# Modulation vectors summed along rows, relative biases written early, and three more up tiles ahead of the expert coefficients, in a three-block model on one Trainium2 core

## Chip, cores and metric

The kernel runs on one core of one Trainium2 chip, in one launch. The metric is the device time in microseconds (us) of that core. Three runs of the kernel before gave 2993.87, 2997.18 and 3000.24 us; the median is 2997.18 us.

## The reference, cut to what matters

256 tokens of width 1024 go through three blocks. The change touches the first block and a small product that the third block uses.

```
# block 1, mixers
z = x @ w_in + b_in                                  # u, v, q, k, v_b and two gates
a = gelu(u) * (tril(w_s) mixed over tokens of LN(gelu(v)) + b_s)
l = q k^T / sqrt(128) + rel_bias[t5_bucket(t - s)]   # 8 heads, causal: NEG_INF where s > t
o = softmax(l) v_b
h = LN(alpha x + (sig(g_a) (a @ w_pa) + sig(g_b) (o @ w_pb)) @ w_out)
# block 1, expert layer: top 16 of 128 x 128 experts for each of 8 heads
hid = gelu(u_tab[experts] . h);  f = sum(gate * hid * v_tab[experts])
e = (p @ w_proj) * sigmoid(h @ w_gate + b_gate)
x = LN(alpha h + f + e)
# block 3: shifts, scales and gates, the same for all tokens
mod = silu(c) @ ada_w[l] + ada_b[l]                  # l = 0, 1: 1024 -> 6144
```

The expert layer is computed densely: all 16384 rows of the up table against all tokens (64 up tiles of 256 experts each), multiplied by a coefficient for each expert and token (zero for those not chosen), and then all 16384 rows of the down table (64 down tiles).

## The kernel before

**Arithmetic.** Most matrix products run as three fp32r products: `wsplit` (L308 to L319) loads 1 MB of weights into one of four `raw` buffers by the SP queue, ScalarE copies it to `hi` (L316), VectorE makes `lo` = raw - hi (L317), and TensorE runs hi x hi, hi x lo, lo x hi (`mm3`, L327 to L329). One chunk is 48 matmuls of 256 columns. An up tile may also be run "whole": 16 plain fp32 matmuls from `raw` (L953), which need no split; each shows as two records. 17 of the 64 up tiles are whole (`WHOLE`).

**Order of the work.** The program is written in one order, but a planner sets each engine's order: it takes instructions by priority (the order of writing) as soon as its own model of the durations says that their inputs and a buffer are there. Every engine then runs its list in order, and the issue of a DMA by ScalarE is an entry in ScalarE's list.

**Mixers of block 1 (`mixers1`, L585).** The values v (four chunks, L605 to L612), layer norm statistics (L613 to L625), normalisation on VectorE (L627 to L630), u (L632 to L636), the token mixing (L645 to L653), then the relative biases: one matmul picks the bias of each distance by head (8 partitions x 256, L658), VectorE copies it into `bv` (8 x 384, masked beyond 256), a DMA writes 128 shifted copies to DRAM from these 8 partitions (`relb`, 1532 KB, L663) and a second DMA reads them back as `rel` (L667), both by ScalarE's queue. Then q and k (L671 to L680), v_b and attention, which adds `rel` (L701).

**Expert layer (`peer`, L838).** `chosen` (L857): queries and scores, then `route` (L776) for two halves of the tokens (top 16, codes; VectorE), with up tiles dealt out between its steps (`run(ups, n)`; a step of an up tile is one sixteenth of it). Then the coefficients: 64 groups of four tokens, each one `bm` (L891) and four `am` (L897) on VectorE, four fp32 matmuls (L898), a copy to `stg` (L899), and one up step; every fourth group writes 1 MB to DRAM (`coef`, L902). 18 up tiles (`GELS`) are emitted by then. `embed` (L909) computes e: one chunk of `w_pp` and four of `w_pg`. In the phase "down" (64 steps, L844 to L848) step j takes the coefficients of tile j from a `slab` (four tiles each, loaded by ScalarE's queue when the first of the four comes up, L971), multiplies (L978), splits, and accumulates down tile j in four PSUM banks; then comes up tile j + 18, and then one `ada.step()`.

**Modulation (L1390 to L1428).** `ada.start` computes silu(c) as 8 columns (L1401). Each of 48 steps loads 128 rows x 2048 columns of `ada_w` (1 MB) and adds them, times the row's silu(c), to an accumulator `adaw` of 128 x 2048 (L1413, L1415). After every eight steps `finish` sums over the partitions: 16 fp32 matmuls of one column (L1426), and adds the bias (L1428).

Of the kernel before, what the change touches and what calls it, by code (L numbers as in the profile page):

```python
# [12 lines left out]
F32 = mybir.dt.float32  # L13
# [4 lines left out]
OP = mybir.AluOpType  # L18
# [4 lines left out]
T = 256  # L23
# [3 lines left out]
LOWEST = -3.0e38  # L27
WCH = 2048
HALFCH = 1024
GELS = 18  # L30
WHOLE = 17
ADDS = 4
LNV = 8
EPS = (1e-6, 1e-5)
# [88 lines left out]
def tcol(v):  # L123

    return np.asarray(v).reshape(-1, 128).T
# [8 lines left out]
def prepare(**a):  # L134
# [6 lines left out]
    for i, n in enumerate(("u", "va", "q", "k", "vb", "ga", "gb")):  # L141
        d["w_" + n] = lay(w[:, i * D:(i + 1) * D], 256)
        if n not in ("va", "vb"):
            vec.add("b_" + n, tcol(b[i * D:(i + 1) * D]))
    d["rows"] = np.stack([b[D:2 * D], b[4 * D:5 * D], a["gmlp_ln_g"][0], a["gmlp_ln_b"][0]])
    d["gm_ws"] = np.ascontiguousarray(a["gmlp_w_s"][0].transpose(2, 0, 1)).reshape(128, -1)
    d["gm_bs"] = a["gmlp_b_s"][0].reshape(1, -1)
    d["w_pa"] = lay(a["w_proj_a"][0], 256)
# [35 lines left out]
    d["rows16"][0] = a["fox_b_f_2"][0]  # L184
    d["rows16"][1] = np.concatenate([a["m_i_bias_3"][0], a["m_f_bias_3"][0]])

    vec.add("c", tcol(a["c_3"][0]))
    for l in range(2):
        d[f"ada{l}"] = np.ascontiguousarray(a["ada_w_3"][l].reshape(KT, 128, 3, WCH).transpose(2, 0, 1, 3))
        vec.add(f"ada_b{l}", tcol(a["ada_b_3"][l]))  # L190
        vec.add(f"n1w{l}", tcol(a["norm1_w_3"][l]))
        vec.add(f"n2w{l}", tcol(a["norm2_w_3"][l]))
# [386 lines left out]
def block1(c, x, ada):  # L579
    with c.phase("mix1", 9):  # L580
        hs = mixers1(c, x)
    ada.start()
    with c.phase("peer", 0):
        return peer(c, x, hs, ada)


def mixers1(c, x):
# [36 lines left out]
    nc.vector.tensor_scalar(sc[:, :, 3:4], sc[:, :, 3:4], -0.5, 1.5, op0=OP.mult, op1=OP.add)  # L624
    nc.vector.tensor_tensor(sc[:, :, 3:4], sc[:, :, 3:4], sc[:, :, 2:3], op=OP.mult)  # L625
    lg, lb = row(2), row(3)
    for i in range(2):  # L627
        nc.vector.tensor_scalar(va[:, i], va[:, i], st[:, i, 12:13], sc[:, i, 3:4], op0=OP.subtract, op1=OP.mult)
        nc.vector.tensor_tensor(va[:, i], va[:, i], lg, op=OP.mult)
        nc.vector.tensor_tensor(va[:, i], va[:, i], lb, op=OP.add)  # L630
# [14 lines left out]
    for g in range(8):  # L645
        ps = c.ms_ps()[:, :256].rearrange("p (n t) -> p n t", n=2)
        for n in range(2):
# [5 lines left out]
        c.split(u[:, g], a[0][:, g], a[1][:, g])  # L653


    L = 383
    ps = c.ms_ps()
    nc.tensor.matmul(ps[:8, :256], c.V("rel_bias")[:32, :], c.C("onehot")[:32, :], start=True, stop=True)  # L658
    bv = c.small([384], tag="bv", bufs=1)
    nc.vector.memset(bv[:8, :], NEG)  # L660
    nc.vector.tensor_copy(bv[:8, :256], ps[:8, :256])
    scr = c.dr.tile([8, 128 * L], F32, name="relb")
    nc.scalar.dma_start(scr.rearrange("h (r l) -> h r l", l=L),  # L663
                        bv[:8, None, :L].to_broadcast([8, 128, L]))
    rel = c.big([8, 256], nm="rel")
    s = scr[:, :]
    nc.scalar.dma_start(rel, bass.AP(tensor=s.tensor, offset=s.offset + 127,  # L667
                                     ap=[[L - 1, 128], [128 * L, 8], [1, 256]]))


    q, k = c.big([KT, T], nm="q"), c.big([KT, T], nm="k")  # L671
    for j in range(4):
        ps = c.lin_chunk(d["w_q"][j], xs)
        for f in range(2):
            h = 2 * j + f
            nc.vector.tensor_scalar(q[:, h], ps[:, f], c.V("b_q")[:, h:h + 1], 128.0 ** -0.5, op0=OP.add, op1=OP.mult)
        ps = c.lin_chunk(d["w_k"][j], xs)
        for f in range(2):
            h = 2 * j + f
            nc.vector.tensor_scalar(k[:, h], ps[:, f], c.V("b_k")[:, h:h + 1], None, op0=OP.add)  # L680
    vb = c.big([2, D], nm="vb")
    bvb = row(1)
    for j in range(4):
# [154 lines left out]
def peer(c, h, hs, ada):  # L838

    scr = c.dr.tile([T // TB, 128, 128 * TB], F32, name="coef")  # L840
    ex = Experts(c, h, hs, scr)
    with c.phase("route", 2, ("r2", "gel")):
        chosen(c, h, hs, ex, scr)
    with c.phase("down", 4, ("r2", "gel")):  # L844
        for j in range(64):
            ex.down(j)
            if j + GELS < 64:
                ex.up(j + GELS)  # L848
            ada.step()
        mean = c.ms_ps()[:, :T]  # L850
        for b in range(4):
            w = h[:, 2 * b:2 * b + 2]
            c.nc.vector.tensor_tensor(w, w, ex.ys[b], op=OP.add)
            for f in range(2):
                c.rows_add(mean, w[:, f], b + f == 0, b + f == 4)
    return c.layer_norm(h, mean, c.V("ln2_g"), c.V("ln2_b"), c.V("ng00"))


def chosen(c, h, hs, ex, scr):
# [26 lines left out]
    for tb in range(T // TB):  # L886
        stg = c.big([128, TB], nm="stg")
        for g in range(0, TB, 4):
            t0 = tb * TB + g
            bm = c.small([4, 128], tag="bm", bufs=3)  # L890
            nc.vector.tensor_tensor(bm, iota[:, None, :].to_broadcast([128, 4, 128]),  # L891
                                    eT[:, 1, t0:t0 + 4, None].to_broadcast([128, 4, 128]), op=OP.is_equal)
            ps = c.ac_ps()
            for i in range(4):
                am = c.small([128], tag="am", bufs=8)
                t = slice(t0 + i, t0 + i + 1)
                nc.vector.tensor_scalar(am, iota, eT[:, 0, t], gT[:, t], op0=OP.is_equal, op1=OP.mult)  # L897
                nc.tensor.matmul(ps[:, i * 128:i * 128 + 128], am, bm[:, i], start=True, stop=True)  # L898
            nc.scalar.activation(stg[:, :, g:g + 4].rearrange("p n t -> p t n"),  # L899
                                 ps.rearrange("p (t n) -> p t n", t=4), AF.Copy)  # L900
            run(ups, 1)
        nc.scalar.dma_start(scr[tb], stg.rearrange("p n t -> p (n t)"))  # L902
    run(ups, 16 * GELS)
    embed(c, h, hs)


def embed(c, h, hs):

    nc, d = c.nc, c.d  # L909
    alpha = 2.0 ** 0.25  # L910
# [5 lines left out]
    for j in range(4):  # L916
        pp = c.mm_ps().rearrange("p (f t) -> p f t", f=2)
        for k in range(2):
            for f in range(2):
                cs = slice((2 * j + f) * 128, (2 * j + f) * 128 + 128)  # L920
                c.mm3(pp[:, f], (w[k][0][:, cs], w[k][1][:, cs]), (pr[0][:, k], pr[1][:, k]), k + f == 0, k == 1,
                      skip_group_check=True)
        pe = c.small([2, T], tag="r2", bufs=6)
        nc.scalar.activation(pe, pp, AF.Copy)
        pg = c.lin_chunk(d["w_pg"][j], hs)
        sg = c.small([2, T], tag="r2", bufs=6)
        for f in range(2):
            g = 2 * j + f
            nc.scalar.activation(sg[:, f], pg[:, f], AF.Sigmoid, bias=c.V("ple_b_gate")[:, g:g + 1])
        nc.vector.tensor_tensor(pe, pe, sg, op=OP.mult)  # L930
        x = h[:, 2 * j:2 * j + 2]
        nc.vector.scalar_tensor_tensor(x, x, alpha, pe, op0=OP.mult, op1=OP.add)


class Experts:
# [26 lines left out]
    def up(self, j):  # L962
        run(self.steps(j), 2 * KT)

    def down(self, j):
        c, nc = self.c, self.c.nc
        b, o = divmod(2 * j, GRP)
        if o == 0:
            self.slabs[b] = c.big([T // TB, GRP, TB], nm="slab")
            src = self.scr[:, :, :]  # L970
            nc.scalar.dma_start(self.slabs[b].rearrange("p a b c -> p a (b c)"),  # L971
                                bass.AP(tensor=src.tensor, offset=src.offset + 2 * j * TB,
                                        ap=[[128 * TB, 128], [128 * 128 * TB, T // TB], [1, GRP * TB]]))
        g = self.gels.pop(j)
        cf = (c.small([2, T], F32R, tag="r2", bufs=6), c.small([2, T], F32R, tag="r2", bufs=6))
        for i in range(2):
# [414 lines left out]
class Modulation:  # L1391
# [1 line left out]


    def __init__(self, c, mod):
        self.c, self.mod = c, mod
        self.cond = c.keep.tile([128, KT], F32, name="cond")
        self.at, self.acc, self.late = 0, None, []

    def start(self):  # L1400
        self.c.nc.scalar.activation(self.cond, self.c.V("c"), AF.Silu)  # L1401

    def step(self):
        c, nc = self.c, self.c.nc
        lg, k = divmod(self.at, KT)
        if lg < 6:
            self.at += 1
            l, g = divmod(lg, 3)
            w = c.wraw(c.d[f"ada{l}"][g, k])
            cond = self.cond[:, k:k + 1]  # L1410
            if k == 0:
                self.acc = c.big(nm="adaw")
                nc.vector.tensor_scalar(self.acc, w, cond, None, op0=OP.mult)  # L1413
            else:
                nc.vector.scalar_tensor_tensor(self.acc, w, cond, self.acc, op0=OP.mult, op1=OP.add)  # L1415
        while self.late:
            self.finish(*self.late.pop(0))
        if lg < 6 and k == KT - 1:
            self.late.append((l, g, self.acc))

    def finish(self, l, g, acc):

        c, nc = self.c, self.c.nc
        cols = c.ms_ps()[:, :16]
        for i in range(16):
            nc.tensor.matmul(cols[:, i:i + 1], acc[:, i * 128:i * 128 + 128], c.C("one")[:, :1], start=True, stop=True)  # L1426
        o = 16 * g
        nc.vector.tensor_tensor(self.mod[:, l, o:o + 16], cols, c.V(f"ada_b{l}")[:, o:o + 16], op=OP.add)  # L1428


def modulated(c, x, sums, w, scale, shift, out=None):
# [608 lines left out]
```

## Time and profile before

| what | us |
|---|---|
| median of three runs | 2997.18 |
| the profiled execution, its own time | 2989.64 |
| its span, first to last instruction | 2987.9 |
| TensorE busy in the span | 2854.9 (96%) |
| VectorE busy | 2060.0 (69%) |
| ScalarE busy | 1547.6 (52%) |
| mixers of block 1 | 0 to about 290 |
| routing and coefficients | about 300 to 556 |
| phase "down" | about 560 to 1233 |

Times in the views are microseconds from the start of the span. A matmul's record is longer than the step from one matmul to the next, since matmuls are pipelined, so the number of records in a stretch says more than the busy time. A wait is listed as "who waited <- for whom". PEclk is the granted TensorE clock as a share of full speed (1.00 is 2.4 GHz, 0.50 is 1.2 GHz). A few per cent of the matmul records can be missing.

### The profile page before, as it was taken

How to read it: one execution, taken by the hardware profiler on the slowest of the kernel's cores; microseconds unless marked ns; L12 is line 12 of the kernel's file. 1: busy time of each engine (PE TensorE's matmuls, PEld its weight loads, DVE VectorE, ACT ScalarE, POOL GpSimd, SP SyncE). 2: the span in 40 equal slices, each digit the busy share in tenths (PEclk: the TensorE clock that was granted, in tenths of full speed). 3: DMA queues.
4: the chain of work that ended last, by engine and by line, in shares of the span. 5: the costliest groups of instructions: out<-in, count | busy, mean ns of one | idle time of the engine just before them, and what ended most of it. 6: DMA issues, size and time to landing. Idle time of an engine off the chain costs nothing. (4 is left out here: it accounts for less than half of the span.)

```text
span 2987.9 us, 51592 instructions
## 1 busy us (share of the span) xinstructions
PE 2854.9 (96%) x21106; PEld 2699.0 (90%) x21106; DVE 2060.0 (69%) x3625; ACT 1547.6 (52%) x2199; POOL 160.8 (5%) x136
## 2 busy tenths in 40 slices
PE   8799999899999999999999999989899999999998
PEld 8699988799999999987899989989899998788886
DVE  6365979776666676577555655555655696899997
ACT  5254417544444444437544464445544555777775
POOL 0000000000000000040000100000100071000000
PEclk9899999999999999999999999989999999999998
DMA  7544345677887796541354424534155432788885
GB/s 262 178 149 171 112 148 221 223 282 278 287 280 277 280 320 231 182 161 48 115 184 171 155 98 142 183 128 172 70 184 186 162 128 99 268 318 333 324 330 216
DMA packets 117709, 601.72 MB, mean 201 GB/s; under 512 B 9688, under 2 KB 45016, under 8 KB 48472
## 3 DMA queue, kind: packets, MB, share of 16 engines
q1 hardware_dynamic: 78480, 557.96, 52.1%
q10 hardware_dynamic: 38984, 40.39, 4.4%
q8 instruction: 167, 2.74, 0.4%
q14 instruction: 78, 0.64, 0.1%
HBM read 578.91 MB, written 19.39 MB: 200 GB/s over the span
## 5 line engine op out<-in xcount | busy, mean ns | idle before, releaser
L317 DVE TENSOR_TENSOR lo<-raw,hi 128x1024 fp32r<-128x1024 f32 x921 | 1130.8, 1243 | 639.0 <-ACT hi L316 635.4
L316 ACT ACTIVATE hi<-raw 128x1024 fp32r<-128x1024 f32 x921 | 966.9, 1057 | 1001.6 <-PE mm L328 519.5
L327 PE MATMUL mm<-nhi,hi 128*128 128x256 f32 x1312 | 379.5, 290 | 10.2 <-ACT nhi L491 6.8
L328 PE MATMUL mm<-nlo,hi 128*128 128x256 f32 x1312 | 379.6, 290 | 0.5 <-DVE nlo L492 0.5
L329 PE MATMUL mm<-nhi,lo 128*128 128x256 f32 x1312 | 377.3, 288 | 0.0
L329 PE MATMUL mm<-lhi,lo 128*128 128x256 f32 x1072 | 306.4, 286 | 8.3 <-DVE lo L317 8.3
L327 PE MATMUL mm<-lhi,hi 128*128 128x256 f32 x1072 | 305.9, 286 | 2.6 <-ACT lhi L454 2.3
L328 PE MATMUL mm<-llo,hi 128*128 128x256 f32 x1072 | 307.2, 287 | 0.0
L328 PE MATMUL ac<-r,hi 128*128 128x256 f32 x1024 | 294.0, 287 | 0.1
L327 PE MATMUL ac<-r,hi 128*128 128x256 f32 x1024 | 294.0, 288 | 0.0
L329 PE MATMUL ac<-r,lo 128*128 128x256 f32 x1024 | 293.3, 287 | 0.0
L327 PEld LDWEIGHTS mm<-nhi,hi 128*128 128x128 f32 x1312 | 258.5, 198 | 12.4 <-ACT nhi L491 7.6
L328 PEld LDWEIGHTS mm<-nlo,hi 128*128 128x128 f32 x1312 | 258.5, 197 | 2.4 <-DVE nlo L492 1.7
L329 PEld LDWEIGHTS mm<-nhi,lo 128*128 128x128 f32 x1312 | 258.3, 197 | 0.1
L329 PEld LDWEIGHTS mm<-lhi,lo 128*128 128x128 f32 x1072 | 207.6, 194 | 10.5 <-DVE lo L317 9.5
L327 PEld LDWEIGHTS mm<-lhi,hi 128*128 128x128 f32 x1072 | 207.7, 194 | 4.4 <-ACT lhi L454 2.9
L328 PEld LDWEIGHTS mm<-llo,hi 128*128 128x128 f32 x1072 | 207.5, 194 | 1.1 <-issue 0.7
L328 PEld LDWEIGHTS ac<-r,hi 128*128 128x128 f32 x1024 | 198.9, 194 | 0.3 <-DVE r L323 0.3
L329 PEld LDWEIGHTS ac<-r,lo 128*128 128x128 f32 x1024 | 198.7, 194 | 0.0
L327 PEld LDWEIGHTS ac<-r,hi 128*128 128x128 f32 x1024 | 198.7, 194 | 0.0
L328 PE MATMUL ac<-hlo,hi 128*128 128x256 f32 x688 | 193.0, 281 | 0.0
L327 PE MATMUL ac<-hhi,hi 128*128 128x256 f32 x688 | 192.8, 280 | 0.0
(592 smaller groups left out, 6285.3 us busy)
## 6 DMA issues: line engine op xcount, KB each, us to landing
raw<-in_moe_gu SPq DMA_DIRECT2D x88, 1024.0 KB, 6.1
raw<-in_peer_u SPq DMA_DIRECT2D x64, 1024.0 KB, 4.9
raw<-in_peer_v SPq DMA_DIRECT2D x64, 1024.0 KB, 5.1
raw<-in_ada SPq DMA_DIRECT2D x48, 1024.0 KB, 7.3
raw<-in_moe_d SPq DMA_DIRECT2D x40, 1024.0 KB, 6.2
raw<-in_up SPq DMA_DIRECT2D x32, 1024.0 KB, 4.9
raw<-in_down SPq DMA_DIRECT2D x32, 1024.0 KB, 4.9
raw<-in_ffn_gu SPq DMA_DIRECT2D x22, 1024.0 KB, 4.9
```

What stands on the lines that cost most here:

```text
L316: nc.scalar.activation(hi, raw[:, a:a + m], AF.Copy)
L317: nc.vector.tensor_tensor(lo, raw[:, a:a + m], hi, op=OP.subtract)
L327: mm(ps, w[0], x[0], start=start, stop=False, **k)
L328: mm(ps, w[0], x[1], start=False, stop=False, **k)
L329: mm(ps, w[1], x[0], start=False, stop=stop, **k)
```

## The change

Four things. (1) `ada_w` is laid out so that a partition is an output column: a step loads 128 columns x 2 x 1024 rows, and VectorE multiplies each half by silu(c), which lies along the row in all partitions, and sums along the row into one column of `mod` (`accum_out`). The accumulators, the column matmuls and `finish` are gone. silu(c) is made at the start of the phase "down" from a broadcast load of 1024 values, and the steps run beside j = 2 to 49. (2) The relative biases are computed before the normalisation of v, for all 128 partitions at once (eight matmuls of 32 rows, four copies on ScalarE), written as two DMAs from 128 partitions (1024 KB, and 508 KB of mask in rows of 127 values), and read back after q and k. (3) `GELS` 18 to 21, `WHOLE` 17 to 20: of every four groups of coefficients three run two up steps and one runs one. (4) `embed` moves into the phase "down", the slab of tile block b + 1 is loaded when block b begins, and the first one within `embed`. Wide buffers of the phase go from 4 to 3, and a scratch area for software DMA is halved.

```
-GELS = 18
-WHOLE = 17
+GELS = 21
+WHOLE = 20
...
     lg, lb = row(2), row(3)
+    L = 383
+    rows, low = c.big([8, 256], nm="relw"), c.small([L - 256], tag="bv", bufs=1)
+    nc.gpsimd.memset(low, NEG)
+    for h in range(0, 8, 2):
+        ps = c.ms_ps().rearrange("p (h l) -> p h l", h=2)
+        for i in range(2):
+            nc.tensor.matmul(ps[:, i], c.V("rel_bias")[:32, h + i:h + i + 1].to_broadcast([32, 128]),
+                             c.C("onehot")[:32, :], start=True, stop=True)
+        nc.scalar.activation(rows[:, h:h + 2], ps, AF.Copy)
+    scr = c.dr.tile([128, 8, L], F32, name="relb")
+    nc.scalar.dma_start(scr[:, :, :256], rows)
+    nc.scalar.dma_start(scr[:, :, 256:], low[:, None, :].to_broadcast([128, 8, L - 256]))
...
-    L = 383
-    ps = c.ms_ps()
-    nc.tensor.matmul(ps[:8, :256], c.V("rel_bias")[:32, :], c.C("onehot")[:32, :], start=True, stop=True)
...
-    nc.scalar.dma_start(scr.rearrange("h (r l) -> h r l", l=L),
-                        bv[:8, None, :L].to_broadcast([8, 128, L]))
-    rel = c.big([8, 256], nm="rel")
...
             nc.vector.tensor_scalar(k[:, h], ps[:, f], c.V("b_k")[:, h:h + 1], None, op0=OP.add)
+    rel = c.big([8, 256], nm="rel")
+    s = scr[:, :, :]
+    nc.scalar.dma_start(rel, bass.AP(tensor=s.tensor, offset=s.offset + 127, ap=[[8 * L - 1, 128], [L, 8], [1, 256]]))
...
-    with c.phase("down", 4, ("r2", "gel")):
+    with c.phase("down", 3, ("r2", "gel")):
+        ada.start()
+        embed(c, h, hs, ex)
         for j in range(64):
             ex.down(j)
             if j + GELS < 64:
                 ex.up(j + GELS)
-            ada.step()
+            if j > 1:
+                ada.step()
...
-            run(ups, 1)
+            run(ups, 1 if g == 12 else 2)
...
+        if j == 2:
+            ex.fetch(0)
         pg = c.lin_chunk(d["w_pg"][j], hs)
...
+        if o == 0 and j < 60:
+            self.fetch(b + 1)
...
     def start(self):
+        self.cond = c.small([D], tag="cond", bufs=1)
+        nc.scalar.dma_start(self.cond, bass.AP(tensor=src.tensor, offset=src.offset + 4 * D, ap=[[0, 128], [1, D]]))
+        nc.scalar.activation(self.cond, self.cond, AF.Silu)
     def step(self):
+        l, q = divmod(self.at, 24)
+        self.at += 1
+        w = c.wraw(c.d[f"ada{l}"][q]).rearrange("p (a k) -> p a k", a=2)
+        for i in range(2):
+            o = 2 * q + i
+            nc.vector.scalar_tensor_tensor(w[:, i], w[:, i], 1.0, self.cond, op0=OP.mult, op1=OP.mult,
+                                           accum_out=self.mod[:, l, o:o + 1])
+        if q == 23:
+            nc.vector.tensor_tensor(self.mod[:, l], self.mod[:, l], c.V(f"ada_b{l}"), op=OP.add)
```

## Rows read from the trace of the kernel before

**Rows 1.** The page's first part: busy time of each engine, its share of the span, instructions.

```profile
PE 2854.9 (96%) x21106; PEld 2699.0 (90%) x21106; DVE 2060.0 (69%) x3625; ACT 1547.6 (52%) x2199; POOL 160.8 (5%) x136
```

**Rows 2.** Stretches of the mixers stage: from and to, length, then busy time (records) of PE, PEld, DVE, ACT and POOL, granted clock, busy share of the DMA engines, GB/s.

```profile
5.00:29.00 24.00, 20.55 (x144) 20.00 (x145) 14.61 (x20) 16.66 (x23) 0.00 (x0) 1.00 1.01 408
40.00:70.00 30.00, 30.00 (x250) 29.40 (x249) 25.14 (x46) 17.02 (x28) 5.87 (x1) 1.00 0.46 168
82.30:104.40 22.10, 0.28 (x3) 0.08 (x1) 0.00 (x1) 1.09 (x2) 0.00 (x0) 0.55 0.44 92
104.40:108.40 4.00, 3.52 (x14) 3.23 (x15) 4.00 (x5) 2.81 (x3) 0.00 (x0) 0.50 1.04 345
```

**Rows 3.** Waits from 0 to 320 us: who waited for whom, us in total, times, longest.

```profile
ACT hi L316 <- DMA relb<-bv: 31.2, 1, 31.2
...
PE mm L327 <- ACT hi L316: 21.8, 1, 21.8
```

**Rows 4.** The instructions that touch `relb`, and the old bias matmul (duration in ns min/median/max, first and last start in us).

```profile
L663 ACTq DMA_DIRECT2D relb<-bv x1: 1276/1276/1276, 67.4 to 67.4; - x1
L667 ACTq DMA_DIRECT2D rel<-relb x1: 390/390/390, 102.8 to 102.8; - x1
...
L658 PE MATMUL ms<-cst,vecs x2: 374/376/378, 65.1 to 65.3; 32*8 32x256 f32 x2
```

**Rows 5.** The instructions that touch `adaw`, in the same columns.

```profile
L1426 PE MATMUL ms<-cst,adaw x192: 164/250/353, 696.1 to 1171.4; 128*128 128x1 f32 x192
L1415 DVE SCALAR_TENSOR_TENSOR adaw<-raw,cond,adaw x42: 2342/2347/2353, 600.1 to 1148.2; 128x2048 f32<-128x2048 f32 x42
L1413 DVE TENSOR_SCALAR adaw<-raw,cond x6: 1279/1281/1287, 584.2 to 1070.2; 128x2048 f32<-128x2048 f32 x6
```

**Rows 6.** TensorE in order of time at the first set of columns: start, length, what.

```profile
695.69 0.28 PE L327 MATMUL mm<-lhi,hi 128*128 128x256 f32 x1
695.81 0.28 PE L328 MATMUL mm<-llo,hi 128*128 128x256 f32 x1
...
696.06 4.12 PE L1426 MATMUL ms<-cst,adaw 128*128 128x1 f32 x32
```

**Rows 7.** Stretches of the phase "down", columns as in rows 2: one of steady work, and the stretch behind each of the six sets of columns.

```profile
600.00:692.00 92.00, 92.00 (x774) 92.00 (x773) 67.16 (x66) 43.69 (x50) 0.00 (x0) 1.00 0.83 297
...
700.10:705.70 5.60, 5.60 (x27) 5.60 (x27) 3.32 (x8) 0.37 (x1) 0.00 (x0) 0.50 0.50 171
798.00:801.40 3.40, 3.40 (x17) 3.40 (x17) 3.31 (x8) 0.00 (x0) 0.00 (x0) 0.50 0.21 60
897.00:900.40 3.40, 3.40 (x19) 3.40 (x18) 3.32 (x9) 0.00 (x0) 0.00 (x0) 0.50 1.01 381
993.50:999.40 5.90, 5.90 (x29) 5.90 (x30) 3.32 (x8) 0.44 (x1) 0.00 (x0) 0.50 0.41 144
1091.50:1095.00 3.50, 3.50 (x18) 3.50 (x18) 3.50 (x10) 0.00 (x0) 0.00 (x0) 0.51 1.00 363
1171.50:1176.90 5.40, 5.40 (x27) 5.40 (x26) 1.91 (x3) 0.00 (x0) 0.00 (x0) 0.50 0.51 164
```

**Rows 8.** Stretches of the routing (410 to 450 us, where TensorE runs whole up tiles alone), of the coefficients, and behind the wait for the first slab, columns as in rows 2.

```profile
410.00:450.00 40.00, 40.00 (x187) 35.17 (x186) 30.63 (x87) 6.46 (x9) 0.00 (x0) 1.00 0.44 150
450.00:515.00 65.00, 64.63 (x451) 58.37 (x450) 64.33 (x198) 48.25 (x52) 0.00 (x0) 1.00 0.56 209
515.00:540.00 25.00, 18.17 (x127) 15.71 (x126) 25.00 (x78) 16.10 (x16) 0.00 (x0) 1.00 0.45 185
540.00:556.00 16.00, 14.29 (x115) 13.50 (x115) 16.00 (x40) 10.44 (x11) 0.00 (x0) 1.00 0.52 198
...
572.30:576.10 3.80, 3.75 (x17) 3.75 (x18) 2.81 (x7) 0.00 (x0) 0.00 (x0) 0.50 0.73 250
```

**Rows 9.** TensorE's groups from 450 to 556 us: line, operation, out <- in, shapes, count, busy us, mean ns, idle before it and for whom.

```profile
L898 PE MATMUL ac<-bm,am 128*128 128x128 f32 x512 | 72.7, 282 | 7.7 <-DVE am L897 7.6
L953 PE MATMUL mm<-x,raw 128*128 128x256 f32 x113 | 31.7, 380 | 0.0
```

**Rows 10.** The writes of `coef` to DRAM (the issue on ScalarE's queue, first and last, and the time to landing).

```profile
L902 ACTq DMA_DIRECT2D coef<-stg x16: 326/326/333, 456.5 to 555.3; - x16
...
DMA to landing us min/median/max: 3.8/4.6/8.2
```

**Rows 11.** Waits from 540 to 580 us, columns as in rows 3.

```profile
DVE gel L978 <- DMA slab<-coef: 6.9, 1, 6.9
PE mm L329 <- DVE lo L317: 6.8, 5, 5.2
```

**Rows 12.** VectorE's groups over the whole span: the split of half a chunk, a multiply-add of 1024 columns, the read of an accumulator (count, busy us, mean ns, idle before).

```profile
L317 DVE TENSOR_TENSOR lo<-raw,hi 128x1024 fp32r<-128x1024 f32 x918 | 1129.8, 1246 | 639.0 <-ACT hi L316 635.4 <-PE mm L329 0.8
...
L1678 DVE SCALAR_TENSOR_TENSOR lg<-hf,lg 128x1024 f32<-128x1024 f32 x2 | 2.4, 1220 | 1.1 <-ACT lg L1677 1.1
...
L1530 DVE DVE_READ_ACCUMULATOR me<-ac,me 128x1 f32 x16 | 1.3, 83 | 0.0
```

**Rows 13.** A ScalarE group from 440 to 600 us: a copy of 512 columns out of PSUM, columns as in rows 12.

```profile
L924 ACT ACTIVATE r<-mm 128x512 f32<-128x512 f32 x4 | 2.4, 598 | 2.5 <-PE mm L329 2.5
```

**Rows 14.** A DMA issue of the first 75 us: a row of values broadcast to all partitions (queue, count, KB each, median us to landing).

```profile
row<-in_rows ACTq DMA_DIRECT2D x2, 512.0 KB, 10.2
```

**Rows 15.** A DMA issue from 600 to 1100 us, in the same columns: the slab loads, which read pieces of 512 bytes.

```profile
slab<-coef ACTq DMA_DIRECT2D x13, 1024.0 KB, 12.1
```

More of the change, by code (lines that the diff above doesn't have):

```diff
@@ L144, in prepare @@
             vec.add("b_" + n, tcol(b[i * D:(i + 1) * D]))
-    d["rows"] = np.stack([b[D:2 * D], b[4 * D:5 * D], a["gmlp_ln_g"][0], a["gmlp_ln_b"][0]])
+    d["rows"] = np.stack([b[D:2 * D], b[4 * D:5 * D], a["gmlp_ln_g"][0], a["gmlp_ln_b"][0],
+                          np.asarray(a["c_3"][0]).reshape(-1)])
     d["gm_ws"] = np.ascontiguousarray(a["gmlp_w_s"][0].transpose(2, 0, 1)).reshape(128, -1)
@@ L185, in prepare @@
     d["rows16"][1] = np.concatenate([a["m_i_bias_3"][0], a["m_f_bias_3"][0]])
-    vec.add("c", tcol(a["c_3"][0]))
     for l in range(2):
-        d[f"ada{l}"] = np.ascontiguousarray(a["ada_w_3"][l].reshape(KT, 128, 3, WCH).transpose(2, 0, 1, 3))
+        d[f"ada{l}"] = np.ascontiguousarray(a["ada_w_3"][l].reshape(D, 24, 2, 128).transpose(1, 3, 2, 0)).reshape(24, 128, WCH)
         vec.add(f"ada_b{l}", tcol(a["ada_b_3"][l]))
@@ L581, in block1 @@
         hs = mixers1(c, x)
-    ada.start()
     with c.phase("peer", 0):
@@ L653, in mixers1 @@
         c.split(u[:, g], a[0][:, g], a[1][:, g])
-    L = 383
-    ps = c.ms_ps()
-    nc.tensor.matmul(ps[:8, :256], c.V("rel_bias")[:32, :], c.C("onehot")[:32, :], start=True, stop=True)
[L659 to L662, printed above, removed]
-    nc.scalar.dma_start(scr.rearrange("h (r l) -> h r l", l=L),
-                        bv[:8, None, :L].to_broadcast([8, 128, L]))
-    rel = c.big([8, 256], nm="rel")
-    s = scr[:, :]
-    nc.scalar.dma_start(rel, bass.AP(tensor=s.tensor, offset=s.offset + 127,
-                                     ap=[[L - 1, 128], [128 * L, 8], [1, 256]]))
     q, k = c.big([KT, T], nm="q"), c.big([KT, T], nm="k")
@@ L900, in chosen, with embed @@
                                  ps.rearrange("p (t n) -> p t n", t=4), AF.Copy)
-            run(ups, 1)
+            run(ups, 1 if g == 12 else 2)
         nc.scalar.dma_start(scr[tb], stg.rearrange("p n t -> p (n t)"))
     run(ups, 16 * GELS)
-    embed(c, h, hs)
-def embed(c, h, hs):
+def embed(c, h, hs, ex):
     nc, d = c.nc, c.d
@@ L963, in up, with fetch @@
         run(self.steps(j), 2 * KT)
+    def fetch(self, b):
+        self.slabs[b] = self.c.big([T // TB, GRP, TB], nm="slab")
+        src = self.scr[:, :, :]
+        self.c.nc.scalar.dma_start(self.slabs[b].rearrange("p a b c -> p a (b c)"),
+                                   bass.AP(tensor=src.tensor, offset=src.offset + b * GRP * TB,
+                                           ap=[[128 * TB, 128], [128 * 128 * TB, T // TB], [1, GRP * TB]]))
     def down(self, j):
@@ L967, in down @@
         b, o = divmod(2 * j, GRP)
[L968 to L973, printed above, removed]
+        if o == 0 and j < 60:
+            self.fetch(b + 1)
         g = self.gels.pop(j)
@@ L1395, in __init__ @@
     def __init__(self, c, mod):
-        self.c, self.mod = c, mod
-        self.cond = c.keep.tile([128, KT], F32, name="cond")
-        self.at, self.acc, self.late = 0, None, []
+        self.c, self.mod, self.at = c, mod, 0
     def start(self):
-        self.c.nc.scalar.activation(self.cond, self.c.V("c"), AF.Silu)
+        c, nc = self.c, self.c.nc
+        src = c.d["rows"]
+        self.cond = c.small([D], tag="cond", bufs=1)
+        nc.scalar.dma_start(self.cond, bass.AP(tensor=src.tensor, offset=src.offset + 4 * D, ap=[[0, 128], [1, D]]))
+        nc.scalar.activation(self.cond, self.cond, AF.Silu)
     def step(self):
+        if self.at == 48:
+            return
         c, nc = self.c, self.c.nc
[L1405 to L1428, printed above, removed]
+        l, q = divmod(self.at, 24)
[7 more added lines that the diff above has]
+            nc.vector.tensor_tensor(self.mod[:, l], self.mod[:, l], c.V(f"ada_b{l}"), op=OP.add)
 def modulated(c, x, sums, w, scale, shift, out=None):
@@ L2028 @@
     arrays, vec_at = prepare(**{k: v for k, v in locals().items()})
-    nc = bacc.Bacc("TRN2", target_bir_lowering=False, num_devices=1)
+    nc = bacc.Bacc("TRN2", target_bir_lowering=False, num_devices=1, dynamic_dma_scratch_size=8192)
     dram = {k: nc.dram_tensor("in_" + k, v.shape, mybir.dt.from_np(v.dtype), kind="ExternalInput").ap()
```

## The prediction

> **What bounds the kernel now.** Over the span it is TensorE, busy 96% [rows 1]; but a busy share hides what is wasted, so I read the three stages that the change touches. In the mixers the stretches show one hole: from 82.3 to 104.4 us TensorE does nothing, and after it the clock is at 0.50 (1.2 GHz) for 4 us [rows 2]. The waits say why: ScalarE waited 31.2 us for the write of `relb` to land, because the read of `rel` stands in its list, and TensorE then waited 21.8 us for ScalarE's split [rows 3]. The write was issued at 67.4 us from 8 partitions, the read could go only at 102.8 us [rows 4]. The difference of the two waits, 31.2 - 21.8 = 9.4 us, is how far ScalarE works ahead of TensorE: a stop of ScalarE shorter than that is free here. In the phase "down" TensorE is full (92.00 of 92 us) with VectorE at 67.16, ScalarE at 43.69 and the DMA engines at 0.83 [rows 7], so there any TensorE work removed is time removed, down to the next limit. In the coefficients VectorE is full from 515 us on (25.00 of 25 us) and TensorE is not (18.17, and a record overstates its step) [rows 8].
>
> **(1) Modulation.** Removed from TensorE: six sets of 16 fp32 column matmuls, 192 records [rows 5]. One set of 32 records takes 4.12 us, standing between split matmuls that step 0.12 us (695.69 to 695.81) [rows 6]; six sets are 24.7 us. Behind each set comes a stretch at half clock, in which TensorE has work throughout. The six stretches add up to 27.2 us and hold 137 records [rows 7]; in steady work a record takes 92/774 = 0.119 us, so these would take 16.3 us: 10.9 us lost. The columns are one wide, and the clock falls right behind every set and not in the 92 us of steady work before the first, so I count the loss as theirs. Together -35.6 us.
>
> Added on VectorE: per step two multiply-adds of 1024 columns with a sum. The nearest rows are a plain multiply-add of that width, 1220 ns, and an accumulator read, 83 ns [rows 12]: 2.61 us, against (42 x 2.347 + 6 x 1.281)/48 = 2.21 us [rows 5]. VectorE needs 67.16/8 = 8.4 us per step of the loop (92 us are eight steps of 11.5 us), so 8.8 us after; TensorE's 96 matmuls take 11.4. Hidden, at 0. The loads are as many and as large.
>
> The steps now end at j = 49 while up tiles end at j = 42, so seven steps (two before) have a down tile and a modulation step alone: TensorE 48 x 0.119 = 5.7 us, VectorE two splits 2.49 [rows 12], the modulation 2.61, and 8.4 - 2.21 - 4 x 1.246 = 1.2 for coefficients and their split, in all 6.3. Five more such steps at 0.6 are 3 us, and 7 if the DMA lags as well; 0 if work done ahead covers it. I take +3.
>
> silu(c) becomes a wait: ScalarE issues a broadcast load and then the activation waits for it, with splits and embed's copies queued behind, for which TensorE waits. A broadcast row took 10.2 us to land [rows 14]; ScalarE's lead is 9.4. Ends 0 and +5 (if half the load is exposed); I take +1.
>
> **(2) Relative biases.** Removed: 22.1 us of idle TensorE, and half of its time at half clock (14 records in 4 us where 1.7 us do), about 1.7 after allowing for the 0.5 idle there: -23.8. Added on TensorE: eight fp32 matmuls of 256 columns, two records each, at 40/187 = 0.214 us a record [rows 8]: 3.4 us, less about 0.5 for the old one [rows 4]: +2.9, at a place where TensorE is full [rows 2]. ScalarE: four copies of 0.598 us [rows 13] and two issues, hidden while it is busy 17.02 of 30 us [rows 2]; VectorE loses a copy; POOL's memset has no one before it.
> The new write is of 1 MB in pieces of 1 KB and 0.5 MB in pieces of 508 bytes. Bounds for it: 1 MB in long pieces lands in 4.6 us [rows 10], 1 MB in pieces of 512 bytes in 12.1 us [rows 15], so 7 to 18 us from an issue at about 43. The planner put the old read about 4.7 us behind the write; if it pulls the new one up in the same way, ScalarE stands for at most 13 us, of which 9.4 are free. So the term lies between -20.9 and -17; emitted after q and k, it can also stand 40 us later and wait for nothing. I take -20.9.
> The Trainium skill ("DMA: Bandwidth & Descriptors", Specifications) asks for 512 bytes at least and says that shorter transfers are read, modified and written; the mask rows are 508. No row shows a price for that; twice the time for that half alone would add about 6 us to the landing, and the sum would not move unless the read stands early.
>
> **(3) Three more up tiles, whole.** TensorE's work grows: a whole tile is 32 x 0.214 = 6.8 us, a split one 48 x 0.119 = 5.7, and three tiles change kind: +3.3. They go where TensorE idles. How much idle there is: by busy time 0.4 + 6.8 + 1.7 = 8.9 us from 450 to 556 [rows 8]; by steps, 512 records of half as many columns at half of 0.214 (an estimate), 113 at 0.214 and some 60 at 0.119 [rows 8, 9] make 86 of 106 us, so 20. Dealing out 7 steps per four groups, instead of 4, gives TensorE 7 x 0.43 + 32 x 0.107 = 6.4 us against VectorE's 6.6 (106/16): nearly even, so hand-over losses appear. The gain is the idle filled less 3.3: between 0 and -16; I take -9. Routing itself is unchanged.
>
> **(4) Embed and slabs.** VectorE stood 6.9 us on the first slab, TensorE 5.4 of it at one time (6.8 in all), and 3.8 us at half clock followed (17 records, 1.8 lost) [rows 8, 11]. The read cannot begin before the last `coef` write has landed (555.3 + 4.6 [rows 10]), nor can the earlier place in the program change that; VectorE's list still holds the splits behind the multiplication. TensorE will have more embed work left by then. Ends 0 and -7; I take -3. Embed's own loads and copies are the same, moved past the load of c only. Later slabs a block ahead take away VectorE waits that TensorE never felt: 0. The smaller scratch area and the third wide buffer free room and issue nothing: 0.
>
> **Sum.** -35.6 + 3 + 1 - 20.9 - 9 - 3 = -64.5 us, from the profiled execution's 2989.6: 2925. That execution lies 7.5 us under the median of the runs shown, from which the same sum gives 2933. I forecast 2930, 2.2% faster.
>
> **Rivals.**
> *A, the bias wait only moves.* If the new write is as slow as the old (about 35 us), with the read pulled up behind it, ScalarE stands again from about 47 us and TensorE loses the same 23.8: 2954. For: the planner misjudged that very write [rows 3, 4], and the weights then move 339 to 408 GB/s before 40 us (the stretch to 29 us has 1.01 of the DMA engines [rows 2]). Against: 128 partitions instead of 8, and the place after q and k.
> *B, "down" hits DMA or VectorE.* Where up tiles have ended, a step moves 2 MB and a quarter slab, 2.36 MB in 5.7 us, 414 GB/s. Steady work needs 297 at a share of 0.83 [rows 7], and it already runs at the pace that is left when the columns go, which speaks against a limit there. If the loop slowed by 15 us in all, 2945. The trace once moved 408 GB/s for 24 us [rows 2]. By the same page of the Trainium skill (Specifications), one core's share of the memory is about 358 GB/s; that row contradicts it. By that figure a late step takes 6.6 us, and the seven would lose about 6.
> *C, slower: the sum along the row is slow.* No row has this sum at 1024 columns with both inputs in memory. VectorE has 11.4 - (8.4 - 2.21) = 5.2 us for a modulation step before it becomes the bound. To eat 64.5 us, 48 steps must exceed that by 1.34: 6.6 us, or 3.3 us for one instruction, 2.5 times the 1.30 of rows 12. At 4 us each the loop gives 48 x 2.8 = 134 us: 3000 or more. The read of 83 ns speaks against it.
>
> **How the numbers follow.** Forecast 0.70, A 0.14, B 0.11, C 0.05. Best case of my terms: -35.6 - 20.9 - 16 - 7 = -79.5, 2910 from the profiled time; the orders that the planner draws elsewhere can move some us either way: low 2904. High: A with its own spread, 2962. A change of 0.2%, 6 us, is about what runs of this kernel can tell from none. Forecast, A and B are all faster: 0.95; C splits into 0.02 same and 0.03 slower.
>
> **What would show it.** No stretch of idle TensorE between 70 and 110 us, and no wait of ScalarE on `relb` over 9 us. No matmul on `adaw`; in steady work of "down" eight steps in about 92 us with no half-clock stretch. `am` matmuls and whole tiles without gaps up to the last `coef`; a wait on the first slab of 0 to 7 us. The sum instruction at 1.2 to 1.3 us. I am wrong if the half-clock stretches stay without the columns, if a new wait of over 10 us appears before 70 us or around 560, or if VectorE ends steps of "down" last.

## The result and the profile after

The changed kernel takes 2927.91 us (median of four runs, 2925.78 to 2931.56) against 2995.52 us: 67.6 us less, ratio 0.9776 with a 95% interval from 0.9756 to 0.9796. The forecast was 2930 us. The profiled execution took 2925.78 us, its span is 2924.1 us.

Where the time went: first the page's busy times of the changed kernel, then its stretches (columns as in [rows 2]).

```profile
PE 2818.6 (96%) x20880; PEld 2666.6 (91%) x20880; DVE 2063.4 (71%) x3757; ACT 1543.8 (53%) x2196; POOL 156.8 (5%) x137
```

```profile
70.00:110.00 40.00, 40.00 (x336) 40.00 (x335) 26.65 (x37) 15.75 (x17) 0.00 (x0) 1.00 0.63 224
...
432.00:537.00 105.00, 105.00 (x746) 99.64 (x746) 104.81 (x311) 73.86 (x76) 0.00 (x0) 1.00 0.62 231
...
547.00:550.40 3.40, 0.64 (x6) 0.44 (x4) 0.00 (x0) 3.35 (x5) 0.00 (x0) 0.99 1.02 358
550.40:560.00 9.60, 5.45 (x29) 5.24 (x30) 5.94 (x12) 2.32 (x3) 0.00 (x0) 0.68 1.06 273
...
575.60:580.00 4.40, 0.89 (x8) 0.68 (x7) 2.52 (x4) 1.71 (x2) 0.00 (x0) 1.00 1.03 277
...
692.00:784.00 92.00, 92.00 (x774) 92.00 (x772) 67.57 (x90) 42.00 (x48) 0.00 (x0) 1.00 0.84 302
1060.00:1110.00 50.00, 50.00 (x422) 50.00 (x422) 43.67 (x60) 22.80 (x27) 0.00 (x0) 1.00 0.89 323
...
1080.00:1100.00 20.00, 20.00 (x171) 20.00 (x170) 18.45 (x25) 9.06 (x11) 0.00 (x0) 1.00 0.96 346
```

The hole of [rows 2] is gone: TensorE is full from 70 to 110 us. The coefficients (432 to 537 us) are now full on TensorE, not only on VectorE [rows 8]; since overlapping records can hide gaps, the part on why the prediction was right counts this again by steps. Steady work of "down" runs at the same step as before (774 records in 92 us [rows 7]), with VectorE at 67.57. What is left are the three holes near 548, 555 and 577 us, around the first slab.

Milestones make the account. The first matmuls that only block 2 has, in the kernel before and in the changed one (duration min/median/max, first and last start):

```profile
L993 PE MATMUL ms<-rraw,cst x14: 592/592/697, 1289.7 to 1342.9; 128*128 128x512 f32 x14
```

```profile
L1001 PE MATMUL ms<-rraw,cst x14: 590/593/697, 1227.6 to 1280.9; 128*128 128x512 f32 x14
```

There the changed kernel leads by 62.1 us, at the end of the span by 63.8. Two earlier milestones are read in the same way: the first expert query, and the first and last coefficient matmul, before and after.

```profile
L898 PE MATMUL ac<-bm,am x512: 272/275/377, 450.2 to 553.8; 128*128 128x128 f32 x171
...
L327 PE MATMUL mm<-lhi,hi x1072: 274/283/581, 299.9 to 1340.3; 128*128 128x256 f32 x179
```

```profile
L901 PE MATMUL ac<-bm,am x512: 270/275/275, 430.8 to 535.4; 128*128 128x128 f32 x171
...
L327 PE MATMUL mm<-lhi,hi x1024: 277/283/580, 280.1 to 1278.3; 128*128 128x256 f32 x171
```

The first expert query starts 19.8 us earlier. The coefficient matmuls end 18.4 us earlier, with three more up tiles done. So 43.7 us are gained between the last coefficient and block 2.

The new pieces, by row. The three DMAs on `relb` (first and last start, landing below), then the sum along the row:

```profile
L638 ACTq DMA_DIRECT2D relb<-bv x1: 618/618/618, 1.0 to 1.0; - x1
L637 ACTq DMA_DIRECT2D relb<-relw x1: 521/521/521, 42.8 to 42.8; - x1
L680 ACTq DMA_DIRECT2D rel<-relb x1: 393/393/393, 78.9 to 78.9; - x1
...
DMA to landing us min/median/max: 5.9/7.4/16.1
```

```profile
L1422 DVE SCALAR_TENSOR_TENSOR raw<-raw,cond x96: 1217/1221/1228, 598.2 to 1106.0; 128x1024 f32<-128x1024 f32 x96
L1422 DVE DVE_READ_ACCUMULATOR raw<-raw,cond x96: 80/83/86, 599.4 to 1107.2; 128x1 f32 x96
```

The bias rows land 5.9 us after 42.8, that is 30 us before they are read (the mask, issued at 1.0 us beside the first loads, took the 16.1); nobody waits on `relb`. The sum costs 1221 + 83 ns. And the waits from 440 to 640 us, which answer to [rows 11]:

```profile
DVE gel L986 <- DMA slab<-coef: 10.5, 2, 8.6
...
PE mm L329 <- DVE lo L317: 7.7, 2, 4.2
...
PE mm L327 <- ACT r L933: 2.8, 1, 2.8
...
ACT cond L1411 <- DMA cond<-in_rows: 1.6, 1, 1.6
```

### The profile page after: what moved, and what is told of

Its sections match the earlier page's. It is cut to its first block, busy times and chain, and to the rows that moved or that the text cites. A ratio compares the mean times of both kernels' runs of the same rounds, so it can differ in the third digit from the quotient of the medians.

```text
span 2924.1 us, 51291 instructions
## 1 busy us (share of the span) xinstructions
PE 2818.6 (96%) x20880; PEld 2666.6 (91%) x20880; DVE 2063.4 (71%) x3757; ACT 1543.8 (53%) x2196; POOL 156.8 (5%) x137
## 5 line engine op out<-in xcount | busy, mean ns | idle before, releaser
L329 PE MATMUL mm<-lhi,lo 128*128 128x256 f32 x1024 | 295.1, 288 | 7.7 <-DVE lo L317 7.7
L327 PE MATMUL mm<-lhi,hi 128*128 128x256 f32 x1024 | 294.9, 289 | 5.1 <-ACT r L933 2.8
L328 PE MATMUL mm<-llo,hi 128*128 128x256 f32 x1024 | 295.6, 289 | 0.0
L328 PE MATMUL ac<-r,hi 128*128 128x256 f32 x1024 | 288.2, 282 | 0.0
L327 PE MATMUL ac<-r,hi 128*128 128x256 f32 x1024 | 287.7, 281 | 0.0
L329 PEld LDWEIGHTS mm<-lhi,lo 128*128 128x128 f32 x1024 | 201.0, 196 | 9.0 <-DVE lo L317 8.1
L327 PEld LDWEIGHTS mm<-lhi,hi 128*128 128x128 f32 x1024 | 201.2, 197 | 6.9 <-ACT r L933 3.0
L328 PEld LDWEIGHTS mm<-llo,hi 128*128 128x128 f32 x1024 | 200.9, 196 | 1.1 <-issue 0.7
L328 PEld LDWEIGHTS ac<-r,hi 128*128 128x128 f32 x1024 | 192.9, 188 | 0.0
L329 PEld LDWEIGHTS ac<-r,lo 128*128 128x128 f32 x1024 | 192.7, 188 | 0.0
L327 PEld LDWEIGHTS ac<-r,hi 128*128 128x128 f32 x1024 | 192.7, 188 | 0.0
```

The lines of the kernel that those rows point to most:

```text
L327: mm(ps, w[0], x[0], start=start, stop=False, **k)
L328: mm(ps, w[0], x[1], start=False, stop=False, **k)
L329: mm(ps, w[1], x[0], start=False, stop=stop, **k)
```

## The experiments

Each is set against the kernel before on its own chip; a difference given in us is of the medians.

**e1, the biases alone.** The kernel before with part 2's lines only.

```
     lg, lb = row(2), row(3)
+    rows, low = c.big([8, 256], nm="relw"), c.small([L - 256], tag="bv", bufs=1)
+    nc.gpsimd.memset(low, NEG)
...
+    nc.scalar.dma_start(scr[:, :, :256], rows)
...
-    ps = c.ms_ps()
-    nc.tensor.matmul(ps[:8, :256], c.V("rel_bias")[:32, :], c.C("onehot")[:32, :], start=True, stop=True)
...
```

> The kernel before with the relative biases alone changed (part 2: computed for 128 partitions before the normalisation of v, read back after q and k); modulation, tiles and slabs as before. Theory (the wait of 31.2 us goes, the new write lands before its read): 18 to 21 us under the kernel before, no stretch of idle TensorE between 70 and 110 us, no half clock there. Rival A (the wait only moves): within 5 us of the kernel before. If the early mask write, which in the changed kernel went out at 1.0 us, costs TensorE the 2 us by which its first matmul came later there, that delay shows here too.

2975.23 against 2992.92 us: 17.7 us, ratio 0.9939 (0.9915 to 0.9962). TensorE is full where the hole was, and nothing waits on `relb`:

```profile
70.00:110.00 40.00, 40.00 (x336) 40.00 (x336) 26.73 (x39) 15.75 (x17) 0.00 (x0) 1.00 0.65 224
```

The gain is just under the 18 to 21 us expected, and its interval is 11 to 25 us; the theory holds, rival A falls. TensorE's first matmul comes at 9.2 us, late as in the changed kernel (8.5; before 6.5); see e8.

**e2, only the read moved.**

```
-    nc.scalar.dma_start(rel, bass.AP(tensor=s.tensor, offset=s.offset + 127,
-                                     ap=[[L - 1, 128], [128 * L, 8], [1, 256]]))
...
             nc.vector.tensor_scalar(k[:, h], ps[:, f], c.V("b_k")[:, h:h + 1], None, op0=OP.add)
+    nc.scalar.dma_start(rel, bass.AP(tensor=s.tensor, offset=s.offset + 127,
+                                     ap=[[L - 1, 128], [128 * L, 8], [1, 256]]))
```

> The kernel before with only the read of the biases written behind q and k in the program; the write still goes from 8 partitions at about 67 us. If the place in the program is what removes the wait: no stop of ScalarE, about 20 us under the kernel before. If the speed of the write is (the planner pulls the read up to where it believes the write has landed): ScalarE still waits 25 to 32 us for relb, TensorE idles about 20 us, and the time is within 5 us of the kernel before. I expect the second.

2990.6 us, ratio 0.9992 (0.9979 to 1.0005): no gain. Its DMAs, and its waits from 0 to 320 us:

```profile
L663 ACTq DMA_DIRECT2D relb<-bv x1: 1276/1276/1276, 67.9 to 67.9; - x1
L678 ACTq DMA_DIRECT2D rel<-relb x1: 390/390/390, 104.2 to 104.2; - x1
```

```profile
ACT hi L316 <- DMA relb<-bv: 26.3, 1, 26.3
...
PE mm L327 <- ACT hi L316: 15.6, 1, 15.6
```

Though written after q and k, the read was put in ScalarE's list only two splits later than before: four stand between the write and the read, where two did. So the place in the program alone does not remove the wait. With the new write (e1) it is gone; whether an early write from 8 partitions, or a late one from 128, would have done it was not tried.

**e3, the modulation alone.** The kernel before with the new class, its layout and its start in "down", steps from j = 0.

```
-    with c.phase("down", 4, ("r2", "gel")):
+    with c.phase("down", 3, ("r2", "gel")):
+        ada.start()
```

> The kernel before with the modulation alone changed (part 1: columns on partitions, sums along the row, silu(c) made at the start of the phase down; steps from j = 0, three wide buffers); biases, tiles and slabs as before. Theory: the 192 column records (24.7 us) and the half clock behind them (10.9 us) both go: 33 to 37 us under the kernel before, no half-clock stretch between 600 and 1180 us. Rival B/C (VectorE or the DMA takes over): under 20 us gained, VectorE at over 90% in steady work of the phase.

2961.16 us: 31.8 us, ratio 0.989 (0.9872 to 0.9908). From 692 us in steady work:

```profile
692.00:784.00 92.00, 92.00 (x774) 92.00 (x773) 67.53 (x89) 42.00 (x48) 0.00 (x0) 1.00 0.84 301
```

VectorE is at 73%, and the granted clock is 1.00 all the way from 600 to 1180 us, so in steady work B and C fall. But the median misses the expected 33 to 37 us (the interval is 27 to 38), and the trace shows why the gain can be smaller. Around the first slab TensorE stops for 7.0 and 4.8 us, 11.7 in all, counted from one matmul's start to the next; in the kernel before it is one stop of 5.4. The waits from 536 to 600 us:

```profile
PE mm L329 <- DVE lo L317: 12.8, 6, 6.7
...
DVE gel L978 <- DMA slab<-coef: 9.1, 2, 8.4
...
DVE raw L1414 <- DMA raw<-in_ada: 2.6, 1, 2.6
```

In the first gap VectorE waits 8.4 us for the slab (6.9 before [rows 11]); the load of c was issued just ahead of it. In the second it waits 2.6 us for a load of `ada_w`, with a split that TensorE needs behind it. Six slab loads go out from 553 to 603 us, three in the kernel before: the accumulators, which shared the wide buffers with the slabs, are gone.

**e4, the same columns, spread.** Two column matmuls a step instead of sixteen at once.

```
-        for i in range(16):
+        for i in range(2 * n, 2 * n + 2):
             nc.tensor.matmul(cols[:, i:i + 1], acc[:, i * 128:i * 128 + 128], c.C("one")[:, :1], start=True, stop=True)
```

> The kernel before with the 16 column matmuls of each group not in one set but two at each of the next eight steps; same number of column matmuls, everything else as before. Theory (the run of one-column matmuls is what lowers the clock): no half-clock stretch between 600 and 1180 us, 10 to 12 us under the kernel before, the 24.7 us of the records kept. Rival (the clock falls for another reason, or the lost time is only the records): the half-clock stretches stay and the time is within 4 us of the kernel before.

2980.06 us: 12.9 us (8 to 17 by the interval), ratio 0.9958 (0.9944 to 0.9973), with not one column matmul removed. The stretch from 600 to 1180 us in the kernel before and in e4:

```profile
600.00:1180.00 580.00, 578.34 (x4746) 578.13 (x4745) 397.35 (x405) 249.69 (x286) 0.00 (x0) 0.97 0.79 283
```

```profile
600.00:1180.00 580.00, 580.00 (x4876) 580.00 (x4876) 407.12 (x415) 258.44 (x295) 0.00 (x0) 1.00 0.81 288
```

So the run of narrow matmuls did lower the clock, and by the medians that is two fifths of what part 1 gains (12.9 of 31.8 us). Around the first slab this trace has one gap of 5.6 us, as before.

**e5, the tiles undone.**

```
-GELS = 21
-WHOLE = 20
+GELS = 18
+WHOLE = 17
...
-            run(ups, 1 if g == 12 else 2)
+            run(ups, 1)
```

> The changed kernel with the tile counts of before (18 up tiles emitted by the coefficients, 17 whole, one step for each group of four tokens). My prediction priced this part at 9 us, between 0 and 16; the trace of the changed kernel has the coefficients no longer than before (105 us) with three more tiles in them, so 48 x 3 split matmuls at 0.119 us leave the phase down for nothing: 17 us, less what the changed start of the phase gives back. Theory: 10 to 17 us slower than the changed kernel (2938 to 2945 us). Rival (the tiles only push the wait on the first slab about): within 5 us of it.

2945.46 us, ratio 0.9847 (0.9833 to 0.986). Against the changed kernel's ratios, 0.9776 and 0.9792 (e9), that is 0.55 to 0.71%, 16 to 21 us; in the traces block 2 starts 13.2 us later (1240.8 us). e6 to e8, which ran on the same chip as e5 and take as long as the changed kernel, had medians of 2926.96 to 2927.32 us, 18 us less. The theory holds; of its 10 to 17 us the trace is inside, the times are at the upper end or above it. From 495 us on the coefficients have the old gap, and they end no sooner (last one at 534.5 us, in the changed kernel at 535.4):

```profile
495.00:521.00 26.00, 18.85 (x129) 16.20 (x128) 26.00 (x81) 16.75 (x16) 0.00 (x0) 1.00 0.46 190
```

**e6, part 4 undone.**

```
-        embed(c, h, hs, ex)
...
+    embed(c, h, hs, ex)
...
-        if o == 0 and j < 60:
-            self.fetch(b + 1)
+        if o == 0:
+            self.fetch(b)
```

> The changed kernel with part 4 undone: embed ahead of the phase down and of the load of c, each slab loaded when its first tile comes up. My prediction gave this part 3 us of gain. The trace of the changed kernel speaks against it: TensorE idles 11.3 us in three gaps around the first slab (6 before), with 13.6 us at half clock (6.8 before), and the second slab is loaded beside the first. Theory now: 3 to 8 us faster than the changed kernel without it (2920 to 2925 us), the first slab landing sooner after its issue. Rival (as predicted): 1 to 5 us slower.

2926.96 us, ratio 0.9783 (0.977 to 0.9796): no difference from the changed kernel that these runs can tell, and the interval is 4 us to either side. My new theory, that the gaps would shrink, was as wrong as the old one. Its waits from 536 to 600 us:

```profile
DVE gel L984 <- DMA slab<-coef: 11.6, 3, 8.9
...
PE mm L329 <- DVE lo L317: 10.9, 2, 7.2
```

Counted from one matmul's start to the next, as in the expectation, the gaps make 11.5 us in two instead of 11.3 in three.

**e7, whole tiles left over for the wait.** `GELS` and `WHOLE` 22.

> The changed kernel with 22 up tiles ahead of the phase down, all 22 whole, dealt out as in the changed kernel, so that 25 of the 352 steps are left when the last coefficient group is done. A whole tile needs no split, hence neither ScalarE's nor VectorE's list. Theory (TensorE idles after the last coefficients because all it has left stands behind the wait for the first slab in VectorE's list): the left-over steps (25 x 0.43 = 10.7 us) cover that wait, the idle of 11 us falls to under 4, the half clock there goes, and the kernel is 6 to 12 us faster than the changed one (2916 to 2922 us). Rival (the DMA, at over 0.9 there, is what the stage waits for): the gaps move behind the left-over steps and the time stays within 4 us.

2927.32 us, ratio 0.9785 (0.9772 to 0.9798): no gain. The idle moved to another list: a whole tile needs no split, but ScalarE still reads its result (`gel`, L963), and that read stood behind the load of c. Waits from 536 to 600 us:

```profile
DVE gel L986 <- DMA slab<-coef: 20.4, 2, 19.3
...
PE mm L327 <- ACT gel L963: 5.2, 1, 5.2
ACT L1411 <- issue: 4.8, 1, 4.8
ACT cond L1411 <- DMA cond<-in_rows: 3.9, 1, 3.9
PE mm L329 <- DVE lo L317: 3.8, 3, 2.7
```

**e8, the mask written late.**

```
-    nc.gpsimd.memset(low, NEG)
+    nc.vector.tensor_scalar(low, rows[:, 0, :L - 256], 0.0, NEG, op0=OP.mult, op1=OP.add)
```

> The changed kernel with the mask tile made from the bias rows on VectorE instead of by POOL's memset, so that its write cannot go out before 42 us (it went at 1.0 us, ahead of the first weights). Theory (the early mask write delays the first loads): TensorE's first matmul at 6.5 us as before the change instead of 8.5 to 9, and 1 to 3 us faster than the changed kernel. Rival (the start varies by itself): first matmul and time unchanged; the mask write may also land late and hold the read.

2927.09 us, ratio 0.979 (0.9771 to 0.9809): the same. TensorE does start at 6.7 us instead of 8.5. In the eight traces with the early mask write it starts at 8.4 to 9.2 us, in the five without at 6.5 to 6.8, so that write did hold up the first loads. But the first expert query starts at 280.0 us, as in the changed kernel (280.1). In this trace a good part of the 1.8 us goes to a stretch at half clock, which the trace of the changed kernel does not have: from 16 to 20 us the granted clock is 0.74, there 1.00. Why it fell here was not tried.

**e9, e10, e11: the changed kernel again, c early, and c early with the left-over tiles.** e10 starts the modulation ahead of the routing:

```
-        eq = c.small([16, NCAND], tag="eq", bufs=2)
+        eq = c.small([16, NCAND], tag="eq", bufs=1)
...
+    ada.start()
     with c.phase("route", 2, ("r2", "gel")):
...
-        ada.start()
```

> The changed kernel once more, on the same chip as the two versions of it below, to set them against: about 2928 us, 0.977 to 0.979 of the kernel before.

> The changed kernel with silu(c) loaded and made ahead of the routing instead of at the start of the phase down (one buffer of the routing's selection instead of two makes the room). Theory (in the gap at 547 us TensorE waited 2.8 us for ScalarE's copies, which stood behind the load of c and two table loads): the first of the three gaps (3.0 us) goes, the other two stay, since they wait for the slab in VectorE's list; 1 to 4 us faster than the changed kernel of this set. Rival (the slab's landing ends the stage whatever stands before it): the gaps grow by what is removed, the time the same.

> As e10, and 22 whole up tiles ahead of the phase down, as in e7. In e7 the left-over steps ran as meant, but then TensorE waited 5.2 us for ScalarE's copy of an up tile, which stood behind the load of c (3.9 us) and its table loads. Theory: without these the left-over steps cover the wait for the slab; TensorE's gaps from 536 to 600 us fall under 5 us in all (11.3 in the changed kernel, 9.6 in e7), and the kernel is 4 to 9 us faster than the changed kernel of this set. Rival: what is saved there is paid by slower whole tiles (two more, 1.1 us each) and by slabs that land late; within 3 us.

e9: 2933.86 us, ratio 0.9792 (0.9772 to 0.9812). e10: 2931.75, 0.9798 (0.9784 to 0.9811). e11: 2928.59, 0.979 (0.9776 to 0.9804). By the ratios none can be told from another. The medians put e11 5.3 us under e9, but e9's own five runs spread over 12.1 us. In e10 the gap near 547 us goes and the next grows from 4.4 to 7.9 us; the gaps make 11.8 us in all. In e11 they make 10.1, and who waits has changed once more (536 to 600 us):

```profile
DVE gel L986 <- DMA slab<-coef: 18.5, 3, 17.4
...
PE mm L327 <- ACT r L933: 3.8, 1, 3.8
PE mm L329 <- DVE lo L317: 3.8, 4, 1.4
```

So e10's rival holds, and e11's theory falls: the gaps were to come under 5 us. Five arrangements (the changed kernel, e6, e7, e10, e11) give TensorE 9.6 to 11.8 us of gaps there. In all of them the first slab is multiplied 15 to 20 us after the last coefficient write was issued, and the lists of VectorE or ScalarE hold what TensorE needs behind it. A version that beats the changed kernel was not found.

## Why the prediction was right

**Part 1, forecast -35.6 + 3 + 1 = -31.6; e3 measured -31.8.** The columns and the clock behind them were read rightly; e4 supports the split (10.9 forecast for the clock, 12.9 measured). That the sum fits as well is in part luck. The +3 for the late steps is not in e3, whose steps begin at j = 0, and in the changed kernel it did not occur: where up tiles have ended (their last matmul starts at 1076 us), TensorE is full, with 171 records from 1080 to 1100 us, 0.117 us each. VectorE is near its limit there (18.45 of 20 us), and the DMA engines moved 346 GB/s, not the 414 of rival B. Work done ahead covered it, the lower end I had kept. In its place the start of the phase cost more than the +1 for c: the gaps around the first slab are 6.3 us longer in e3. With that, -35.6 + 6.3 gives -29.3, and from the last coefficient matmul to block 2 e3's trace is 29.4 us shorter than the one before (706.5 against 735.9). The load of c is not all of it, since e10 takes c away and keeps 11.8 us of gaps. The prediction had the change of the wide buffers at 0, because it was to "free room and issue nothing"; with the accumulators gone, the slab loads went out sooner. That their crowding makes the second gap is read from the waits of e3, not tried.

**Part 2, forecast -20.9; e1 measured -17.7 (11 to 25 by its interval), the milestone -19.8.** The bias rows landed in 5.9 us. My bounds of 7 to 18 were for both halves together; in e8, where the two writes go out within 3.3 us of each other, the second lands 11.8 us after the first was issued, inside them. The read stood far behind. Not foreseen was the start: POOL's memset, free at once, let the mask write go ahead of the first weights (e8).
The Trainium skill's 512 bytes ("DMA: Bandwidth & Descriptors", Specifications) fit e8, but e8 does not show that they are the cause: 508 KB of mask in pieces of 508 bytes took 9.1 us to land and 1024 KB in pieces of 1 KB took 8.5. Per byte that is twice the time, as my sentence on it had supposed. Both writes have 1024 pieces, though, so a fixed time for each piece would give the same. It fell outside the path.

```profile
relb<-relw ACTq DMA_DIRECT2D x1, 1024.0 KB, 8.5
relb<-bv ACTq DMA_DIRECT2D x1, 508.0 KB, 9.1
```

**Part 3, forecast -9, between 0 and -16; e5 measured 13 to 21.** This term was mis-sized. I took the middle of the range for fear of hand-over losses between VectorE and TensorE. There are hardly any: between the first and the last coefficient matmul no step from one matmul's start to the next is over 0.22 us, where in the kernel before those over 0.3 us added up to 14 us. The stage lasts 104.6 us where it lasted 103.6. The bound by steps was the value to take. It was a little high itself: the coefficient records step 0.112 us, not the estimated 0.107, which leaves 17 us of idle instead of 20, and less 3.3 that is about 14. The bound by busy time (8.9) was misleading, because a record of 282 ns covers gaps between steps of 112.

**Part 4, forecast -3, between 0 and -7; e6 measured 0, with 4 us of interval.** The prediction said that the place in the program cannot move the first read ahead of the last write's landing, and that holds. The -3 rested on TensorE having more embed work left: it had, and it stands behind the same wait. The gaps around the first slab even grew, from 5.4 us to 11.3, and one sign of the prediction failed with that: VectorE's wait on the first slab was to be 0 to 7 us and is 8.6 (10.5 with that on a later one). The growth does not come from part 4. It is there with the old tiles (e5, 10.0), with the old embed and slabs (e6, 11.5), and with part 1 alone (e3, 11.7), and it is absent with part 2 alone (e1, 5.5): it comes with part 1.

The terms sum to -31.8 - 17.7 - 13 (to 21) + 0 = -62 to -71 us, against -67.6 measured. The forecast of -64.5 came so near because its errors offset each other: parts 2 and 4 gave about 3 us less each than forecast, part 3 gave 4 to 12 more. C was right to be small: the sum took 1.30 us, just as its two rows said [rows 12].

## What to carry to other kernels

Price a stage's idle by counting steps, not by busy time, when records overlap. A DMA that reads back what another has written wants that write early and quick; moving the read in the program is not enough where a planner sets the order (e2). A change that only frees buffers is not free of effect either: here the loads that could use them went out sooner (e3). Filling an engine's idle was worth nearly its full size here until the engine was full; then the next hand-over, the first read of the coefficients, kept what was left, whichever list was cleared.

## What the runs showed of the hardware that was not expected

Sixteen matmuls of one column in a row, 4.12 us [rows 6], cost another 2 us behind them by the clock, which in the first set fell before the set had ended (0.87 from 695.9 to 700.1 us). Two of them between 96 wide ones cost nothing of that kind: e4's granted clock is 1.00 over 580 us. TensorE is busy throughout in both (578.34 and 580.00 of 580 us).

A write of 1532 KB from 8 partitions took about 35 us to land (67.4 to 102.8 us [rows 4]), one of 1024 KB from 128 partitions 5.9 us. Other traffic was not what held the first: from 91 to 102 us, when the loads beside it had landed, the DMA engines moved about 50 GB/s at a busy share of 0.4. Whether the 8 partitions do it, or the source row that is read 128 times, no run separates.
